# A hybrid decoder trunk on one core: square roots and inverse square roots move from Newton steps on VectorE to a power operation on GpSimd

## The chip, the cores and the metric

The kernel runs on one core of one Trainium2 chip. The metric is the device time of one execution, in microseconds (us). Engines carry the profile's names: PE (TensorE, matrix products), DVE (VectorE), ACT (ScalarE), POOL (GpSimd) and SP (SyncE, which starts most DMAs); PEld is the loading of weights into PE.

## The reference

Two layers over 16 meta tokens and 512 sequence tokens with 1024 channels, all in float32. Each layer is a feed-forward block, a mixer of three parallel groups that share one input and one output projection, and a second feed-forward block, each followed by a normalization. The places with a square root or its inverse are these:

```python
def _layer_norm(x, g, b):
    mu = jnp.mean(xf, axis=-1, keepdims=True)
    var = jnp.mean(jnp.square(xf - mu), axis=-1, keepdims=True)
    return (xf - mu) * lax.rsqrt(var + LN_EPS) * g + b
def _rms_norm(x, w):
    return xf * lax.rsqrt(jnp.mean(xf * xf, axis=-1, keepdims=True) + RMS_EPS) * w
def _l2norm(x):
    return x * lax.rsqrt(jnp.sum(x * x, axis=-1, keepdims=True) + RMS_EPS)
# _rg_lru_group, for each of 256 channels and every token
    a = jnp.exp(log_a)
    b = jnp.sqrt(-jnp.expm1(2.0 * log_a)) * (i * u)
    _, h = lax.associative_scan(_linear_combine, (a, b), axis=1)
# one layer
    h = _layer_norm(ALPHA * h + 0.5 * _swiglu(h, ...), ...)
    lru, ssd, dn = split(h @ w_in)
    mix = concatenate([_rg_lru_group(lru), _ssd_group(ssd), _deltanet_group(dn)]) @ w_out
    h = _layer_norm(ALPHA * h + mix, ...)
    h = _layer_norm(ALPHA * h + 0.5 * _swiglu(h, ...), ...)
```

The state-space group ends in an rms norm, the delta group l2-normalizes its q and k and ends in an rms norm, and the recurrent group (RG-LRU) takes the square root of a whole array.

## The kernel before

Activations lie with channels on the 128 partitions and tokens along the free dimension. The tokens are cut into two units: u=0 with 272 tokens (16 meta and 256) and u=1 with 256. Every large product is done as three float32r products of high and low parts (`hh`, `hl` for activations, `wt` for weights). A weight slab of 128x1024 arrives by DMA in `wr` (3 buffers), ACT writes its high part into `wt` (6 buffers), and the low part is a subtraction, for about 70% of the mixer's slabs and the shared feed-forward slabs in four parts on POOL (`wt<-wr,wt 128x256`), otherwise in one piece on DVE (`wt<-wr,wt 128x1024`). Products land in PSUM tiles `g` (3 buffers), all small products in PSUM tiles `c` (5 buffers).

Nothing is issued while the program is written down. A `Recorder` collects every operation with what it reads and writes, prices it (`price`, line 117), and `schedule` (line 233) sets one order for each engine: of the operations that are ready, the one with the longest priced path to the end goes first. `issue` then emits that order, so nearly all instructions carry line 390 in the profile and are told apart by their tiles. Each engine is handed its instructions in that order; what it needs from another engine it waits for with a semaphore, and what stands behind a waiting instruction on DVE or POOL waits with it. A POOL operation with two inputs is priced, whatever its arithmetic, at `148 + 2.1 * n` ns for n elements per partition (line 150): 719 ns for 272.

The two units are staggered, so that the mixer of one runs beside the feed-forward block of the other (`weave`). In the profile the stretches from about 300 to 900 us and from about 1560 to 2200 us hold the mixers of layers 0 and 1; the rest is almost pure feed-forward.

`rsqrt` (line 782) is eleven DVE instructions: two integer instructions on the bits for a first guess, then three Newton rounds of three instructions, each depending on the one before. It is called 42 times, on these tiles:

- `lv` in `layer_norm` (10 calls; 3 elements per partition). Behind it PE spreads the result over the partitions, and all 8 pieces of `acc` are scaled by it.
- `d_ss` in `dn_pre` (10 calls; 4 or 2 elements), followed by a product with `s0`, which makes a square root; it scales `v`.
- `d_sq` in `dn_finish` (4 times two calls in a row; 12 elements for u=0 and 8 for u=1), then spread by PE over the delta group's output.
- `s_sv` in `ssd_finish` (4 calls; 6 or 4 elements).
- `lru` in `lru` (8 calls: 2 layers, 2 units, 2 halves k; 272 or 256 elements). The argument is `r`, the guess is in `th`, and the scratch is the tile `l_h`, so that the Newton rows read `l_h<-lru`, `l_h<-l_h,lru` and `lru<-l_h,lru`. A POOL product with `r` makes the square root, then DVE forms the gated input (`lru<-lru`) and scans it (`l_h<-lru`, into `l_h`). The working tile `lru` has one buffer, so the second half starts when the first is done.
- `frs` in `final_tile` (2 calls; 2 elements), for the last normalization, done in rows.

`dn_finish`, `ssd_finish` and the two halves of `lru` all stand ahead of a unit's output projection, which reads all three groups. Below, these four stretches (two layers, two units) are called the finishes. `softplus`, a helper for other places, computes log(1+e) with a series of about a dozen DVE instructions.

Of the kernel before, what the change touches and what calls it, by code (L numbers as in the profile page):

```python
# [10 lines left out]
I32 = mybir.dt.int32  # L11
# [4 lines left out]
P = 128  # L16
# [383 lines left out]
class Trunk:  # L400
# [29 lines left out]
    def consts(self):  # L430
        nc, ins = self.nc, self.ins
        self.ident = self.tl(self.cp, [P, P], "ident")
        nc.gpsimd.memset(self.ident, 0.0)
        nc.gpsimd.affine_select(self.ident, self.ident, compare_op=ALU.not_equal, fill=1.0, base=0, pattern=[[-1, P]], channel_multiplier=1)
        self.hh = [self.tl(self.hp, [P, KD, n], f"hh{u}", F32R) for u, n in enumerate(NTOK)]
        self.hl = [self.tl(self.hp, [P, KD, n], f"hl{u}", F32R) for u, n in enumerate(NTOK)]
        self.acc = [None, None]
        self.res = [self.tl(self.dr, [P, KD, n], f"res{u}") for u, n in enumerate(NTOK)]
        self.par = self.tl(self.cp, [P, NROW], "par")
        self.ones = self.tl(self.cp, [P, P], "ones")  # L440
        nc.gpsimd.memset(self.ones, 1.0)
        nc.idle = self.ones
        self.tri = self.tl(self.cp, [P, P], "tri")
        nc.gpsimd.affine_select(self.tri, self.ones, pattern=[[1, P]], compare_op=ALU.is_ge, fill=0.0, base=0, channel_multiplier=-1)
        self.bd = self.block_ones(64, "bd")
        self.bdtri = self.tl(self.cp, [P, P], "bdtri")
        nc.gpsimd.tensor_tensor(self.bdtri, self.tri, self.bd, ALU.mult)
        self.tri2 = self.fold(self.bdtri, "tri2")
        self.eye2 = self.fold(self.ident, "eye2")
        self.mask = []  # L450
        for k in (16, 32):
            m = self.block_ones(2 * k)
            v = m.rearrange("p (b c) -> p b c", c=2 * k)
            nc.gpsimd.memset(v[:, :, :k], 0.0)
            nc.gpsimd.affine_select(m, m, pattern=[[2 * k, P // (2 * k)], [0, 2 * k]], compare_op=ALU.is_ge, fill=0.0, base=k - 1, channel_multiplier=-1)
            self.mask.append(self.fold(m, f"mask{k}"))
        self.bd16 = self.fold(self.block_ones(16), "bd16")
        self.pm = self.tl(self.cp, [P, 1], "pm")
        nc.vector.tensor_reduce(self.pm, self.eye2[:, 0:META], axis=AX.X, op=ALU.add)
        self.halo = self.tl(self.cp, [P, 14, 3], "halo")  # L460
        self.lcar = self.tl(self.cp, [P, 2], "lcar")

# [316 lines left out]
        assert f0 == NF  # L779
        return shared, alone  # L780

    def rsqrt(self, y, v, tmp):

        nc = self.nc
        nc.vector.tensor_scalar(y.bitcast(I32), v.bitcast(I32), 1, None, ALU.logical_shift_right)
        nc.vector.tensor_scalar(y.bitcast(I32), y.bitcast(I32), -1, 0x5F3759DF, ALU.mult, ALU.add)
        for _ in range(3):
            nc.vector.tensor_tensor(tmp, y, y, ALU.mult)
            nc.vector.scalar_tensor_tensor(tmp, tmp, -0.5, v, ALU.mult, ALU.mult)
            nc.vector.scalar_tensor_tensor(y, tmp, 1.5, y, ALU.add, ALU.mult)  # L790

    def layer_norm(self, u, s, row, off=0, keep=False):

# [33 lines left out]
            nc.vector.tensor_scalar(v[:, 0, 1:nb], vp[:, 1:nb], 1.0 / D, LN_EPS, ALU.mult, ALU.add)  # L827
        else:
            nc.vector.tensor_scalar(v[:, 0, :nb], vp[:, :nb], 1.0 / D, LN_EPS, ALU.mult, ALU.add)
        self.rsqrt(v[:, 1, :], v[:, 0, :], v[:, 2, :])  # L830
        rp = self.tl(self.psm, [P, 512], "c")[:, :n]
        for i, (c, w) in enumerate(blocks):
            nc.tensor.matmul(rp[:, c:c + w], v[:w, 1, i:i + 1].to_broadcast([w, P]), self.ident[:w, :w], start=True, stop=True)
# [171 lines left out]
    def dn_pre(self, u, bi, st):  # L1005
# [42 lines left out]
        nc.vector.tensor_scalar(tmp, cb, -1.0, None, ALU.mult)  # L1048
        nc.vector.tensor_tensor(nn, nn, tmp.unsqueeze(3).to_broadcast([P, 2, nch, 64]), ALU.mult)
        nc.gpsimd.tensor_tensor(kq[:, :, :, 1], kq[:, :, :, 1], eg, ALU.mult)  # L1050
        self.rsqrt(irk, s0, tmp)
        nc.vector.tensor_tensor(irk, irk, s0, ALU.mult)
        dn = self.tl(self.dr, [2, 16448], "d_nd", bufs=3)
        for h in range(2):
            dst = dn[h, :16384].rearrange("(a j c t) -> a j c t", j=2, c=2, t=64)
# [155 lines left out]
    def dn_finish(self, l, u, st):  # L1211
        nc = self.nc
        n = NTOK[u]
        bl = self.blocks(u)
        nb = len(bl)
        sq = st["sq"]
        ot = [st["big"][:, 6 + p, :n] for p in range(2)]
        qs = []
        for p in range(2):
            q = self.tl(self.wk, [P, 272], "lq")[:, :n]  # L1220
            nc.scalar.activation(q, ot[p], AF.Square)
            qs.append(q)
        po = self.tl(self.psm, [P, 512], "c")
        for p in range(2):
            for bi, (o, w) in enumerate(bl):
                nc.tensor.matmul(po[:w, bi * 4 + 2 * p:bi * 4 + 2 * p + 2], qs[p][:, o:o + w], self.bd[:, 0:128:64], start=True, stop=True)
        for bi, (o, w) in enumerate(bl):
            nc.vector.tensor_copy(sq[:w, bi, 1], po[:w, bi * 4:bi * 4 + 4])
        T = lambda i: sq[:, :nb, i]
        rq, a2, tmp = T(2), T(3), T(4)  # L1230
        nc.vector.tensor_scalar(T(0), T(0), RMS_EPS, None, ALU.add)
        self.rsqrt(rq, T(0), tmp)
        nc.vector.tensor_scalar(rq, rq, 0.125, None, ALU.mult)
        nc.vector.tensor_tensor(a2, rq, rq, ALU.mult)
        nc.vector.scalar_tensor_tensor(a2, a2, 1.0 / 64, T(1), ALU.mult, ALU.mult)
        nc.vector.tensor_scalar(a2, a2, RMS_EPS, None, ALU.add)
        self.rsqrt(T(0), a2, tmp)
        nc.vector.tensor_tensor(rq, rq, T(0), ALU.mult)
        for p in range(2):
            rb = self.bcast_rows(u, lambda bi, w: [sq[:w, bi, 2, 2 * p + h:2 * p + h + 1] for h in range(2)])  # L1240
            nc.vector.scalar_tensor_tensor(ot[p], ot[p], self.col(ROW_DNW + l), rb, ALU.mult, ALU.mult)
        for p in range(2):
            nc.vector.tensor_tensor(ot[p], ot[p], st["gate"][p], ALU.mult)
            self.out_split(u, 6 + p, ot[p])
# [82 lines left out]
    def ssd_finish(self, l, u, st):  # L1327
# [13 lines left out]
            for bi, (o, w) in enumerate(bl):  # L1341
                nc.tensor.matmul(po[:w, bi * 2 + g:bi * 2 + g + 1], q[0][:, o:o + w], self.ones[:, 0:1], start=True, stop=True)
        sv = self.tl(self.mx, [P, 3, 3, 2], "s_sv", bufs=2)
        v, y, tmp = (sv[:, i, :nb] for i in range(3))
        nc.vector.memset(v, 1.0)
        for bi, (o, w) in enumerate(bl):
            nc.vector.tensor_scalar(v[:w, bi], po[:w, bi * 2:bi * 2 + 2], 0.25 / 256, RMS_EPS, ALU.mult, ALU.add)
        self.rsqrt(y, v, tmp)
        for g in range(2):
            rb = self.bcast_rows(u, lambda bi, w: [sv[:w, 1, bi, g:g + 1]])  # L1350
            for j in (2 * g, 2 * g + 1):
# [3 lines left out]
    def lru(self, l, u, k, uc):  # L1355
# [18 lines left out]
        nc.gpsimd.tensor_tensor(r, a, a, ALU.mult)  # L1374
        nc.vector.scalar_tensor_tensor(r, r, 1.0, th, ALU.add, ALU.mult)
        nc.vector.tensor_scalar(r, r, -1.0, 1e-37, ALU.mult, ALU.max)
        self.rsqrt(th, r, uc)
        nc.gpsimd.tensor_tensor(r, r, th, ALU.mult)
        nc.vector.scalar_tensor_tensor(i, i, 0.5, r, ALU.mult, ALU.mult)
        nc.vector.tensor_tensor_scan(uc, a, i, 0.0 if u == 0 else self.lcar[:, k:k + 1], ALU.mult, ALU.add)  # L1380
        if u == 0:
# [167 lines left out]
    def final_tile(self, u, m):  # L1549
# [15 lines left out]
        if m < KD - 1:  # L1565
            return
        v = self.tl(self.wk, [P, 2, 2], "fmv")
        w = self.tl(self.wk, [P, 4, 2], "frs")
        for b in range(2):
            nc.vector.bn_aggr(v[:, b], st[:, b])  # L1570
        var, r, t, mr = (w[:, i] for i in range(4))
        nc.vector.tensor_scalar(var, v[:, :, 1], LN_EPS, None, ALU.add)
        self.rsqrt(r, var, t)
        g, o = self.gb[:, :D], self.gb[:, D:]
        nc.vector.scalar_tensor_tensor(mr, v[:, :, 0], -1.0, r, ALU.mult, ALU.mult)
        nc.scalar.activation(x[1], x[1], AF.Identity, scale=r[:, 1:2], bias=mr[:, 1:2])
# [64 lines left out]
```

## Time and profile before

| | us |
|---|---|
| median of 3 runs | 2460.74 (2446.69 to 2464.13) |
| the profiled execution's own time | 2460.38 |
| span of its trace | 2458.7 |
| busy: PE, DVE | 2312.6, 1504.2 |
| busy: ACT, POOL | 865.9, 883.0 |

The span reaches from the first to the last instruction; 1.7 us of the profiled execution's time lie around it. Busy shares are averages over stretches with different limits, and a busy PE is not PE at its peak.

### The profile page before, as it was taken

To read this page: it belongs to the slowest core of one execution; us is meant where nothing else is said; L and a number is where in the kernel's file an instruction comes from. 1 tells how busy PE (TensorE), PEld (TensorE's weight loads), DVE (VectorE), ACT (ScalarE), POOL (GpSimd) and SP (SyncE) were. 2 spreads that over 40 slices of the span, in tenths; PEclk is the share of its full clock that TensorE was granted. 3 is DMA by queue.
4 is the path that set the end of the run, shared out by engine and by line. 5 is a ranking of instruction groups with operands and counts; after the bars stand their busy time and mean duration, and the time that the engine had idled before them with its cause. 6 is when DMAs were issued, how large, how long until landed. Compare 5 with 4: busy or idle time off the path is not lost.

```text
span 2458.7 us, 46832 instructions
## 1 busy us (share of the span) xinstructions
PE 2312.6 (94%) x18712; PEld 2199.1 (89%) x18712; DVE 1504.2 (61%) x3529; ACT 865.9 (35%) x1546; POOL 883.0 (36%) x1214
## 2 busy tenths in 40 slices
PE   8999998988899999999999999998989989999997
PEld 8999998876887999999999999988768878999996
DVE  6444467757867664444574444678577686654445
ACT  3222344442333454222242223443433444432222
POOL 5000566634545576000010005666445556640000
PEclk9999999987886999999999999999888989999999
DMA  6232454531341456233232334545314525552320
GB/s 169 78 103 87 131 145 144 146 97 35 110 108 54 139 157 186 86 104 95 68 95 80 91 91 138 156 139 141 97 35 118 142 61 155 172 168 90 91 90 35
DMA packets 426332, 271.99 MB, mean 111 GB/s; under 512 B 33421, under 2 KB 407921, under 8 KB 425857
## 3 DMA queue, kind: packets, MB, share of 16 engines
q1 hardware_dynamic: 425536, 268.83, 37.7%
q8 instruction: 147, 2.41, 0.4%
q0 software_dynamic: 576, 0.16, 0.1%
q14 instruction: 73, 0.59, 0.1%
HBM read 260.76 MB, written 8.19 MB: 109 GB/s over the span
## 4 chain that ended last, share of the span: by engine, by line
PE 70%; DVE 16%; DMA 4%; issue 3%; POOL 3%; ACT 3%; SPq 0%; POOLq 0%; DVEq 0%; ACTq 0%
PE g L390 61%; PE c L390 9%; POOL wt L390 2%; DVE wt L390 2%; DVE acc L390 2%; DVE fs L390 1%; DVE lru L390 1%; ACT wt L390 1%; DMA wr<-in_ffn_w_gate_dram 1%; DVE d_sq L390 1%; DVE s L390 1%; DMA wr<-in_ffn_w_up_dram 1%; DMA d_tx<-d_xd 1%; DVE sp L390 1%; DVE l_h L390 1%
## 5 line engine op out<-in xcount | busy, mean ns | idle before, releaser
L390 PE MATMUL g<-hh,wt 128*128 128x256 f32 (+1 forms) x7616 | 1063.7, 290 | 22.5 <-DVE fs L390 8.8
L390 PEld LDWEIGHTS g<-hh,wt 128*128 128x128 f32 x7616 | 985.4, 192 | 37.5 <-DVE fs L390 9.0
L390 POOL TENSOR_TENSOR wt<-wr,wt 128x256 fp32r<-128x256 f32 x884 | 681.8, 803 | 783.7 <-ACT wt L390 726.4
L390 ACT CAST wt<-wr 128x1024 fp32r<-128x1024 f32 x484 | 498.0, 1040 | 619.0 <-PE g L390 482.0
L390 PE MATMUL g<-hl,wt 128*128 128x256 f32 (+1 forms) x3808 | 562.7, 288 | 1.8 <-DVE hl L390 1.2
L390 PE MATMUL g<-hid,wt 128*128 128x256 f32 (+1 forms) x4224 | 543.7, 286 | 18.6 <-DVE hid L390 10.2
L390 PEld LDWEIGHTS g<-hid,wt 128*128 128x128 f32 x4224 | 524.4, 189 | 27.2 <-DVE hid L390 13.0
L390 PEld LDWEIGHTS g<-hl,wt 128*128 128x128 f32 x3808 | 505.3, 192 | 6.3 <-DVE hl L390 2.5
L390 DVE SCALAR_TENSOR_TENSOR acc<-g,acc 128x256 f32<-128x256 f32 (+1 forms) x608 | 256.7, 427 | 226.1 <-PE g L390 222.0
L390 DVE TENSOR_TENSOR wt<-wr,wt 128x1024 fp32r<-128x1024 f32 x263 | 335.0, 1285 | 88.1 <-ACT wt L390 86.8
L390 DVE SCALAR_TENSOR_TENSOR fs<-ft,g 128x272 f32<-128x272 f32 (+1 forms) x200 | 84.6, 423 | 188.8 <-ACT ft L390 188.0
L390 DVE TENSOR_TENSOR g<-fs,g 128x256 f32<-128x256 f32 (+1 forms) x176 | 76.4, 434 | 173.9 <-PE g L390 173.5
L390 ACT ACTIVATE ft<-g 128x272 f32<-128x272 f32 (+1 forms) x208 | 80.6, 388 | 281.6 <-PE g L390 249.2
L390 ACT CAST hid<-g 128x256 fp32r<-128x256 f32 (+1 forms) x176 | 65.8, 374 | 223.5 <-DVE g L390 223.2
L390 POOL TENSOR_TENSOR ls<-ls,lq 128x256 f32<-128x256 f32 (+1 forms) x30 | 27.6, 920 | 264.2 <-ACT lq L390 261.3
L390 DVE TENSOR_TENSOR hid<-g,hid 128x256 fp32r<-128x256 f32 (+1 forms) x176 | 74.9, 425 | 42.4 <-ACT hid L390 42.1
L390 POOL TENSOR_TENSOR wr<-wr,db 128x512 f32<-128x512 f32 x4 | 5.0, 1274 | 262.0 <-ACT wr L390 262.0
L390 DVE SCALAR_TENSOR_TENSOR fs<-g,par,fs 128x271 f32<-128x271 f32 (+1 forms) x144 | 69.1, 482 | 21.9 <-ACT halo L390 17.0
L390 ACT ACTIVATE fs<-g,par 128x272 f32<-128x272 f32 (+1 forms) x48 | 25.2, 524 | 67.4 <-PE g L390 57.9
L390 DVE SCALAR_TENSOR_TENSOR acc<-acc,par,c 128x256 f32<-128x256 f32 (+1 forms) x104 | 43.6, 480 | 8.6 <-PE c L390 8.5
L390 ACT ACTIVATE ft<-fs 128x272 f32<-128x272 f32 (+1 forms) x56 | 23.7, 423 | 58.6 <-DVE fs L390 58.6
L390 POOL TENSOR_TENSOR s<-s,s_sm 128x512 f32<-128x512 f32 (+1 forms) x20 | 22.0, 1105 | 61.6 <-ACT s L390 45.1
(305 smaller groups left out, 1742.4 us busy)
## 6 DMA issues: line engine op xcount, KB each, us to landing
wr<-in_ffn_w_gate_dram SPq DMA_DIRECT2D x120, 512.0 KB
wr<-in_ffn_w_up_dram SPq DMA_DIRECT2D x120, 512.0 KB
wr<-in_ffn_w_down_dram SPq DMA_DIRECT2D x120, 512.0 KB
wr<-in_w_in_dram SPq DMA_DIRECT2D x88, 512.0 KB
wr<-in_w_out_dram SPq DMA_DIRECT2D x32, 512.0 KB
res<-acc SPq DMA_DIRECT2D x2, 1088.0 KB
acc<-res SPq DMA_DIRECT2D x8, 272.0 KB
acc<-in_x_dram SPq DMA_DIRECT2D x4, 512.0 KB
```

The lines of the kernel that those rows point to most:

```text
L390: op.fn(*[on(x) for x in op.args], **{k: on(x) for k, x in op.kw.items()})
```

## The change

`rsqrt` is gone. `power` is one POOL instruction with two inputs: the argument, and a tile `half` that holds the exponents 0.5 and -0.5 in its two columns, one of them repeated along the free dimension. The inverse square roots take -0.5. The two places that multiplied an inverse square root by its argument to get a square root (`d_ss` and `lru`) take 0.5 and drop that product, which was a DVE instruction in `dn_pre` and a POOL instruction in `lru`. Prices and rules of the `Recorder` are the same, so the power is priced like any POOL operation with two inputs.

```diff
+        self.half = self.tl(self.cp, [P, 2], "half")
+        nc.gpsimd.memset(self.half[:, 0:1], 0.5)
+        nc.gpsimd.memset(self.half[:, 1:2], -0.5)
...
-    def rsqrt(self, y, v, tmp):
-
-        nc = self.nc
-        nc.vector.tensor_scalar(y.bitcast(I32), v.bitcast(I32), 1, None, ALU.logical_shift_right)
-        nc.vector.tensor_scalar(y.bitcast(I32), y.bitcast(I32), -1, 0x5F3759DF, ALU.mult, ALU.add)
-        for _ in range(3):
-            nc.vector.tensor_tensor(tmp, y, y, ALU.mult)
-            nc.vector.scalar_tensor_tensor(tmp, tmp, -0.5, v, ALU.mult, ALU.mult)
-            nc.vector.scalar_tensor_tensor(y, tmp, 1.5, y, ALU.add, ALU.mult)
+    def power(self, y, v, e):
+
+        t = self.half[:, 0 if e > 0 else 1:][:v.shape[0], 0:1]
+        for _ in v.shape[2:]:
+            t = t.unsqueeze(2)
+        self.nc.gpsimd.tensor_tensor(y, v, t.to_broadcast(list(v.shape)), ALU.pow)
...
-        self.rsqrt(v[:, 1, :], v[:, 0, :], v[:, 2, :])
+        self.power(v[:, 1, :], v[:, 0, :], -0.5)
...
-        self.rsqrt(irk, s0, tmp)
-        nc.vector.tensor_tensor(irk, irk, s0, ALU.mult)
+        self.power(irk, s0, 0.5)
...
-        self.rsqrt(rq, T(0), tmp)
+        self.power(rq, T(0), -0.5)
...
-        self.rsqrt(T(0), a2, tmp)
+        self.power(T(0), a2, -0.5)
...
-        self.rsqrt(y, v, tmp)
+        self.power(y, v, -0.5)
...
-        self.rsqrt(th, r, uc)
-        nc.gpsimd.tensor_tensor(r, r, th, ALU.mult)
+        self.power(r, r, 0.5)
...
-        self.rsqrt(r, var, t)
+        self.power(r, var, -0.5)
```

The order that the planner sets is new on every engine, since it depends on the prices. Two places show it. The numbers behind a tile's name only tell buffers apart; they are one higher after the change, because `half` was allocated ahead of them.

DVE before, in the finish of layer 0, u=0: the second half of the LRU (`lru`, `l_h_950`) with the delta group's norm (`d_sq`) and the state-space group's (`s_sv`).

```order
L390 SCALAR_TENSOR_TENSOR lru_944<-l_h_950,lru_944 128x272
L390 TENSOR_SCALAR d_sq_653<-d_sq_653 128x3x4
L390 TENSOR_TENSOR s_sv_1036<-s_sv_1036 128x6
L390 TENSOR_TENSOR l_h_950<-lru_944 128x272
L390 TENSOR_SCALAR d_sq_653<-d_sq_653 128x3x4
L390 SCALAR_TENSOR_TENSOR s_sv_1036<-s_sv_1036 128x6
L390 SCALAR_TENSOR_TENSOR l_h_950<-l_h_950,lru_944 128x272
L390 SCALAR_TENSOR_TENSOR fs_138<-g_139,par_103,fs_138 128x256
L390 SCALAR_TENSOR_TENSOR lru_944<-l_h_950,lru_944 128x272
L390 SCALAR_TENSOR_TENSOR fs_138<-g_139,par_103,fs_138 128x256
```

The Newton rounds of the three tiles are dealt out in turn, one instruction of each, with a convolution row (`fs`) between.

DVE after, at the same place, from the instruction that ends the LRU's argument (`TENSOR_SCALAR lru`) on.

```order
L390 TENSOR_SCALAR lru_945<-lru_945 128x272
L390 TENSOR_TENSOR d_sq_654<-d_sq_654 128x3x4
L390 MEMSET s_sv_1037 128x6
L390 SCALAR_TENSOR_TENSOR d_sq_654<-d_sq_654 128x3x4
L390 TENSOR_SCALAR s_sv_1037<-c_125 16x2
L390 TENSOR_SCALAR s_sv_1037<-c_125 128x2
L390 SCALAR_TENSOR_TENSOR fs_148<-ft_138,g_146 128x272
L390 TENSOR_SCALAR s_sv_1037<-c_125 128x2
L390 TENSOR_SCALAR d_sq_654<-d_sq_654 128x3x4
L390 SCALAR_TENSOR_TENSOR lru_945<-lru_945 128x272
L390 TENSOR_TENSOR d_sq_654<-d_sq_654 128x3x4
L390 SCALAR_TENSOR_TENSOR l_h_951<-lru_945 128x272
```

The rounds are gone. The instruction that reads the root (`SCALAR_TENSOR_TENSOR lru<-lru`) stands eight rows behind the one that ends its argument, and the second norm of `d_sq`, the scan into `l_h` and all that follows stand behind it.

POOL before, at the same place: weight parts, one product for the LRU (`lru`) and copies for the next unit (`mt`).

```order
L390 TENSOR_TENSOR wt_156<-wr_132,wt_156 128x256 x2
L390 TENSOR_TENSOR lq_577<-lq_577,lq_576 128x272
L390 TENSOR_TENSOR lru_944<-lru_944 128x272
L390 TENSOR_TENSOR wt_156<-wr_132,wt_156 128x256 x2
L390 COPY mt_719<-sm_623 16x128 x3
L390 TENSOR_TENSOR wt_158<-wr_120,wt_158 128x256 x4
L390 TENSOR_TENSOR wt_133<-wr_134,wt_133 128x256 x4
L390 TENSOR_TENSOR lru_944<-lru_944 128x272
L390 COPY lcar_118<-l_h_950 128x1
```

The LRU appears with a product ahead of its root and one behind it; the norms do not appear.

POOL after, at the same place.

```order
L390 TENSOR_TENSOR wt_134<-wr_133,wt_134 128x256 x2
L390 TENSOR_TENSOR d_sq_654<-d_sq_654,half_117 128x3x4
L390 TENSOR_TENSOR wt_134<-wr_133,wt_134 128x256
L390 TENSOR_TENSOR lru_945<-lru_945 128x272
L390 TENSOR_TENSOR lq_578<-lq_578,lq_577 128x272
L390 TENSOR_TENSOR wt_143<-wr_135,wt_143 128x256
L390 TENSOR_TENSOR lru_945<-lru_945,half_117 128x272
L390 TENSOR_TENSOR s_sv_1037<-s_sv_1037,half_117 128x6
L390 TENSOR_TENSOR d_sq_654<-d_sq_654,half_117 128x3x4
L390 TENSOR_TENSOR wt_143<-wr_135,wt_143 128x256 x2
L390 COPY lcar_119<-l_h_951 128x1
L390 TENSOR_TENSOR wt_143<-wr_135,wt_143 128x256
```

Rows with `half` are powers. The LRU's power of 272 elements stands directly ahead of the powers of `s_sv` and of the second `d_sq`, and behind these wait the weight parts.

## Rows read from the trace of the kernel before

**Rows 1.** The page, part 1: span, then busy us (share) and instructions of each engine.

```profile
span 2458.7 us, 46832 instructions
PE 2312.6 (94%) x18712; PEld 2199.1 (89%) x18712; DVE 1504.2 (61%) x3529; ACT 865.9 (35%) x1546; POOL 883.0 (36%) x1214
```

**Rows 2.** The page, part 4: shares of the span on the chain that ended last, by engine.

```profile
PE 70%; DVE 16%; DMA 4%; issue 3%; POOL 3%; ACT 3%; SPq 0%; POOLq 0%; DVEq 0%; ACTq 0%
```

**Rows 3.** The chain in the four finishes, shares by tile: 586-626, 786-822, 1815-1870, 1990-2045 us.

```profile
by line: DVE lru L390 25.0%; DVE d_sq L390 22.6%; DVE l_h L390 14.4%; issue 7.6%; DVE wt L390 5.9%; DVE fs L390 5.7%; POOL acc L390 4.2%; DVE s_sv L390 2.7%; PE c L390 2.5%; POOL lru L390 1.9%; DVE db L390 1.8%; DVE acc L390 1.7%; DVE s_st 
by line: PE g L390 24.9%; PE c L390 22.0%; DVE lru L390 10.6%; DVE d_sq L390 10.3%; DVE s_sv L390 8.3%; DVE l_h L390 8.0%; DVE wt L390 3.2%; PE g L388 3.0%; DVE lv L390 2.8%; issue 1.9%; DVE fs L390 1.7%; DVE ls L390 1.6%; DVE hid L390 1.0%
by line: PE g L390 28.7%; PE c L390 18.0%; DVE d_sq L390 13.1%; DVE lru L390 9.9%; DVE l_h L390 6.4%; DVE acc L390 4.1%; DVE wt L390 4.1%; DVE fs L390 3.6%; POOL wt L390 3.5%; ACT wt L390 1.7%; DVE db L390 1.7%; DVE s_sv L390 1.1%; DVE sp L
by line: DVE d_sq L390 13.3%; PE g L390 12.5%; DVE lru L390 12.2%; DVE l_h L390 11.5%; DVE acc L390 9.2%; DVE hl L390 8.7%; issue 6.6%; DVE lv L390 5.8%; DVE fs L390 5.2%; DVE wt L390 4.9%; ACT wt L390 1.9%; PE c L390 1.6%; DVE s_sv L390 1.
```

**Rows 4.** Waits of PE: tile waited for, us in total, times, longest.

```profile
PE c L390 <- DVE lv L390: 9.3, 6, 2.3
PE c L390 <- DVE d_sq L390: 4.4, 2, 3.2
PE c L390 <- DVE s_sv L390: 2.8, 2, 1.4
```

**Rows 5.** DVE groups of small calls: form, count, busy us, mean ns, idle before.

```profile
L390 DVE SCALAR_TENSOR_TENSOR lv<-lv 128x3 f32<-128x3 f32 x60 | 13.7, 229 | 1.2
L390 DVE TENSOR_TENSOR lv<-lv 128x3 f32<-128x3 f32 x30 | 6.8, 228 | 0.5
L390 DVE TENSOR_SCALAR lv<-lv 128x3 int32<-128x3 int32 x20 | 7.9, 397 | 0.4
L390 DVE SCALAR_TENSOR_TENSOR d_sq<-d_sq 128x12 f32<-128x12 f32 (+1 forms) x52 | 17.1, 328 | 0.3
L390 DVE TENSOR_TENSOR d_sq<-d_sq 128x12 f32<-128x12 f32 (+1 forms) x32 | 8.2, 255 | 0.2
L390 DVE TENSOR_SCALAR d_sq<-d_sq 128x12 int32<-128x12 int32 (+3 forms) x28 | 11.5, 412 | 0.1
L390 DVE SCALAR_TENSOR_TENSOR d_ss<-d_ss 128x4 f32<-128x4 f32 (+1 forms) x60 | 14.8, 260 | 0.4
L390 DVE TENSOR_TENSOR d_ss<-d_ss 128x4 f32<-128x4 f32 (+1 forms) x40 | 9.7, 256 | 0.4
L390 DVE TENSOR_SCALAR d_ss<-d_ss 128x4 f32<-128x4 f32 (+3 forms) x40 | 9.3, 253 | 0.1
```

**Rows 6.** DVE groups of the LRU's Newton steps, same columns.

```profile
L390 DVE SCALAR_TENSOR_TENSOR l_h<-l_h,lru 128x272 f32<-128x272 f32 (+1 forms) x24 | 12.9, 540 | 0.1
L390 DVE SCALAR_TENSOR_TENSOR lru<-l_h,lru 128x272 f32<-128x272 f32 (+1 forms) x24 | 12.3, 511 | 0.2
L390 DVE TENSOR_TENSOR l_h<-lru 128x272 f32<-128x272 f32 (+1 forms) x24 | 12.1, 505 | 0.4
L390 DVE TENSOR_SCALAR lru<-lru 128x272 f32<-128x272 f32 (+3 forms) x32 | 15.8, 493 | 1.6 <-ACT lru L390 1.5
```

**Rows 7.** POOL groups, same columns: weight parts, the LRU's products, a one-column copy.

```profile
L390 POOL TENSOR_TENSOR wt<-wr,wt 128x256 fp32r<-128x256 f32 x884 | 681.8, 803 | 783.7 <-ACT wt L390 726.4 <-PE g L390 34.4 <-issue 13.0
L390 POOL TENSOR_TENSOR lru<-lru 128x272 f32<-128x272 f32 (+1 forms) x16 | 12.3, 769 | 36.1 <-DVE lru L390 13.7 <-ACT lru L390 11.5 <-DVE d_sq L390 8.6
L390 POOL COPY lcar<-l_h 128x1 f32<-128x1 f32 x4 | 0.8, 204 | 3.3 <-DVE d_sq L390 2.6 <-DVE l_h L390 0.6
```

**Rows 8.** Timeline in the first finish: start us, duration us, engine, operation, count.

```profile
605.33 3.28 DVE L390 SCALAR_TENSOR_TENSOR lru<-lru 128x272 f32<-128x272 f32 x1
605.52 2.79 POOL L390 TENSOR_TENSOR wt<-wr,wt 128x256 fp32r<-128x256 f32 x4
```

**Rows 9.** Tile `lru` over the span: length, busy us (count) of DVE, ACT, POOL; clock, DMA.

```profile
0.00:2459.00 2459.00, 96.31 (x152) 14.64 (x32) 12.30 (x16) 0.95 0.38 111
```

**Rows 10.** All work from 600 to 700 us: length, busy of PE, PEld, DVE, ACT, POOL; clock.

```profile
600.00:700.00 100.00, 89.95 (x692) 84.56 (x691) 88.54 (x274) 41.36 (x84) 56.59 (x81) 0.90 0.43 117
```

More of the change, by code (lines that the diff above doesn't have):

```diff
@@ L1229, in dn_finish @@
         T = lambda i: sq[:, :nb, i]
-        rq, a2, tmp = T(2), T(3), T(4)
+        rq, a2 = T(2), T(3)
         nc.vector.tensor_scalar(T(0), T(0), RMS_EPS, None, ALU.add)
-        self.rsqrt(rq, T(0), tmp)
+        self.power(rq, T(0), -0.5)
         nc.vector.tensor_scalar(rq, rq, 0.125, None, ALU.mult)
@@ L1343, in ssd_finish @@
         sv = self.tl(self.mx, [P, 3, 3, 2], "s_sv", bufs=2)
-        v, y, tmp = (sv[:, i, :nb] for i in range(3))
+        v, y = (sv[:, i, :nb] for i in range(2))
         nc.vector.memset(v, 1.0)
@@ L1567, in final_tile @@
         v = self.tl(self.wk, [P, 2, 2], "fmv")
-        w = self.tl(self.wk, [P, 4, 2], "frs")
+        w = self.tl(self.wk, [P, 3, 2], "frs")
         for b in range(2):
             nc.vector.bn_aggr(v[:, b], st[:, b])
-        var, r, t, mr = (w[:, i] for i in range(4))
+        var, r, mr = (w[:, i] for i in range(3))
         nc.vector.tensor_scalar(var, v[:, :, 1], LN_EPS, None, ALU.add)
-        self.rsqrt(r, var, t)
+        self.power(r, var, -0.5)
         g, o = self.gb[:, :D], self.gb[:, D:]
```

## The prediction

> **What bounds the kernel now.** I read part 1 of the page first: PE is busy for 94% of the span, DVE for 61% and POOL for 36% [rows 1]. So only the time in which PE stands still or its work comes late can be won. The chain that ended last, next, is PE for 70% of the span and DVE for 16% [rows 2], so DVE work does lie on the path. Where, the chain by stretches shows: in the finishes, where a unit's three groups end ahead of the output projection [rows 3]. There the tiles of the changed code carry large shares. Last come the waits of PE: it stands idle 9.3 us in all for `lv`, 4.4 for `d_sq` and 2.8 for `s_sv` [rows 4]. In the pure feed-forward stretches none of this bounds anything. In the stretch of the first finish DVE is busy 88.5 of 100 us and POOL 56.6 [rows 10].
>
> **What is removed.** For the small tiles I add up the groups of rows 5. `lv`: 13.7 + 6.8 + 7.9 = 28.4 us for 10 calls. `d_sq`: 48 of the 52, 24 of the 32 and 16 of the 28 instructions are Newton's, 15.8 + 6.2 + 6.6 = 28.6 us for 8 calls. `d_ss`: all of the first two groups and 20 of the 40 in the third, 14.8 + 9.7 + 4.7 = 29.2 us for 10 calls. `s_sv` and `frs` are 66 more instructions; at 0.23 us, the lowest mean of rows 5, 15 us for 6 calls. Together 101 us for 34 calls, 3.0 us each. For the LRU it is 12.9 + 12.3 + 12.1 and half of 15.8, 45.2 us for 8 calls, 5.65 us each [rows 6]. So DVE loses 146 us of its 1504, and POOL loses 8 products at 0.77 us [rows 7].
>
> **What of it lies on the path.** The four finishes of rows 3 are 40, 36, 55 and 55 us long. Share by length gives 9.0 + 3.7 + 7.2 + 7.3 = 27 us of chain for `d_sq`, 44 us for `lru` and `l_h` together (25.9 + 18.5), and about 5 us for `s_sv`. Of the `d_sq` rows about three quarters are Newton's (28.6 of 36.8 us), so 20 us. Of DVE's 96.3 us on the tile `lru` [rows 9], 45.2 are Newton's; `l_h` has other rows too, so I take two fifths of 44, 18 us. For `lv` I take what PE waits, 9.3 us. The small tiles then have 20 + 5 + 9.3 = 34 us on the path and the LRU 18. `d_ss` I cost at nothing: its root only scales `v`, and the block inverses through DRAM stand between that and its use; without that cover it would be worth a few us more.
>
> **What is added.** 42 POOL instructions that no trace here shows. Nearest are a one-column copy, 0.20 us, and a product of two inputs over 272 columns, 0.77 us [rows 7]; the second is the lower end for the LRU's power. A power done in software takes a logarithm, a product and an exponential. The kernel's own `softplus` spends about a dozen DVE steps on one logarithm; with as many for the exponential and some handling of bits I count up to 30 passes, and 30 at 0.77 us are 23 us, the upper end by rows. A loop that keeps its intermediate values in registers need not pay the loads and stores of 30 passes. Newton's 11 steps would be 8.5 us as POOL passes, and a general power does more than these. I take 12 us for 272 columns, between 8.5 and 23 and nearer the lower, which is 44 ns per column; 12 columns would then be about 0.7 us, 3 columns about 0.3 us.
>
> The Trainium skill has a rule that bears on this price (GPSIMD Engine Reference, Elementwise — side-by-side cycle accounting): a loop with three or more operations per element runs at roughly three operations a cycle. By it, 30 operations are 10 cycles of 1.2 GHz per column, an estimate of 2.3 us for 272 columns, and the sum would be that of the first rival. No run here shows it for more than one operation.
>
> **The small powers.** Power and hand-over: 0.3 to 0.7 us, and about half of a weight part that is already running, 0.4 of 0.8 us [rows 7]; 1.1 us in place of 3.0. On the path that turns 34 us into 13: a gain of 21 us. Both ends: nothing, if the power waits behind a whole slab of four parts (3.2 us), and 34 us, if it costs nothing.
>
> **The LRU's powers.** Here the order matters. The planner prices the power at 0.72 us, like a product, and places the DVE instruction that reads the root accordingly: in the piece of DVE's order shown, eight mostly small rows behind the end of the argument. In seven of the eight places there are only none to eight such rows, about 1.2 us of work on average; in one (layer 0, u=1, first half) about 9 us. Everything behind that reader on DVE stands too: the scan, the second `d_sq` norm, the accumulations from PSUM. On POOL, the powers of `s_sv` and `d_sq` and the weight parts queue behind the long power. At 12 us DVE stands for 7 x 10.8 + 3 = 79 us. Not all of it moves the end: DVE holds from under half to most of the chain in the finishes [rows 3], and I count two thirds, 52 us. Less the 18 us of Newton rows that leave, the LRU costs 34 us net.
>
> **The sum.** 2460.4 us of the profiled execution, which is 0.3 below the median of the runs, less 21, plus 34: 2474 us. The same sum with other prices of the LRU's power (each at two thirds): 0.77 us gives 2421, 5 us 2439, 8 us 2453, 18 us 2506, 23 us 2533. It is zero at about 9.5 us. So the whole forecast hangs on one number that the trace does not hold, and the change trades a certain gain at the small tiles for an open cost at the large one.
>
> **The rivals.**
>
> *The power is cheap*, a few passes: 0.8 to 5 us for 272 columns. For it speaks that a sum over one instruction has one load and one store, whereas Newton's eleven steps pay these eleven times: the `lv` steps take 0.23 us on three columns [rows 5]. Against it speaks that POOL takes 0.77 us for a single product, so that even one pass is slower than on DVE (0.50 to 0.54 us, rows 6). The times run from 2421 to 2439; I put it at 2428.
>
> *The power is dear*: one LRU power holds POOL for 23 us or more. It decides from about 14 us on, where 1% is lost, and at 23 us DVE stands 7 x 21.8 + 14 = 167 us; two thirds of that give 2533 and all of it 2588, since with POOL blocked that long the weight parts come late as well and PE has no other work. I put it at 2555. For it: a software power is the only POOL operation here that is not one simple arithmetic step. Against it: nothing in the trace; it would be odd only to plan such an instruction at 0.72 us.
>
> *POOL holds DVE off*, even from rows that need nothing of it. In the first finish a DVE instruction that reads two tiles in SBUF takes 3.28 us, where like instructions of the Newton steps take 0.54 [rows 6], and it spans four POOL weight parts of 2.79 us [rows 8]. If a power holds DVE off in the same way, the rows placed beside it no longer hide any of it: DVE stands 8 x 12 = 96 us for the LRU, two thirds of it 64 in place of 52, and the 34 small powers stop DVE for some 0.5 us each, 17 us of which I count two thirds. That is 2474 + 12 + 11 = 2497. The Trainium skill states this as a rule (SBUF — State Buffer, SBUF: two separate sides): a DVE instruction with two SBUF inputs and a POOL instruction that reads SBUF share a port pair, and whichever starts first blocks the other for its whole length. The trace agrees in this row; whether a power that mostly computes holds the port too, no run here shows.
>
> **How the numbers follow.** I give the forecast (a power of 5 to 18 us, the loss and the gain of like size) 0.37, the cheap power 0.31, the dear one 0.22 and the held-off DVE 0.10. The forecast's own range is 2439 to 2506. A measurement of this kernel can tell about 1% from no change, so the bounds are 2436 and 2485. Faster by more than that: 0.28 of the cheap case and 0.03 of the forecast, 0.31. Within: 0.20 of the forecast, 0.03 of the cheap case and 0.02 of the held-off one, 0.25. Slower: 0.14, 0.22 and 0.08, 0.44. The range for 8 in 10 runs from 2412, where all of the small tiles' 34 us goes and the LRU's power hides, to 2620, beyond 2588 since a power somewhat above 23 us is not excluded; a loop that works lane by lane would lie far above, and is most of what I leave out.
>
> **What would show it.** In the changed kernel's profile: a POOL group of 8 powers on `lru` with its mean, which settles the main term (12 us expected; under 5 the cheap rival, over 20 the dear one); POOL groups of powers on `lv`, `d_sq`, `d_ss` and `s_sv` of 0.3 to 0.7 us; DVE busy near 1360 us, more if it is held off; idle time of DVE ahead of `lru<-lru`, released by POOL, near 79 us in all; in the finishes `d_sq` gone from the chain; PE's waits for `lv` down to a third. The forecast is wrong in its main step if the LRU's power is under 5 us or over 18. It is wrong in its counting if the power is near 12 us and the time still moves by more than 2%, for then DVE's standing counts by much more or less than two thirds.

## The result, and the profile after

The changed kernel takes 2712.4 us (median of 4 runs, 2708.2 to 2721.9), the kernel before 2458.2 us beside it: a ratio of 1.1048, with a 95% interval of 1.1012 to 1.1084. By that ratio it is some 258 us slower, where the forecast was 14 us slower and the range ended at 2620 us.

The page of the changed kernel: part 1 (busy us, share, instructions), three rows of part 2 (tenths in 40 slices of the span) and the head of part 4 (the chain by engine).

```profile
span 2709.5 us, 46251 instructions
...
PE 2286.2 (84%) x18614; PEld 2179.7 (80%) x18614; DVE 1412.7 (52%) x3057; ACT 865.7 (32%) x1546; POOL 1255.0 (46%) x1250
...
PE   9999999843994499999999999999339834999997
...
POOL 4001776489558877000000026664887488860000
PEclk9999999875897699999999999998669867999999
...
PE 48%; POOL 16%; issue 14%; DVE 13%; DMA 5%; ACT 3%; SPq 0%; POOLq 0%; DVEq 0%; ACTq 0%
```

DVE lost 91.5 us of work [rows 1], and POOL, which had 3% of the chain [rows 2], now has 16%. PE was at nine tenths almost everywhere; now it is busy for only three to four tenths in slices 9 and 10, 13 and 14, 29 and 30, and 33 and 34. These are the four finishes. In them the granted clock is low as well, 0.5 to 0.7.

What POOL does there, in its groups of powers (form, count, busy us and mean ns, idle before), then the DVE group that reads the LRU's root and one that waited for another POOL product:

```profile
L390 POOL TENSOR_TENSOR lru<-lru,half 128x272 f32<-128x272 f32 x4 | 175.2, 43790 | 1.4 <-DVE s_sv L390 1.1 <-DVE lru L390 0.2
L390 POOL TENSOR_TENSOR lru<-lru,half 128x256 f32<-128x256 f32 x4 | 164.7, 41184 | 6.5 <-DVE lru L390 3.4 <-DVE d_sq L390 3.1
...
L390 POOL TENSOR_TENSOR d_sq<-d_sq,half 128x12 f32<-128x12 f32 x4 | 9.2, 2302 | 0.3 <-DVE d_sq L390 0.3
...
L390 POOL TENSOR_TENSOR lv<-lv,half 128x3 f32<-128x3 f32 x10 | 8.7, 872 | 7.5 <-DVE lv L390 7.5
...
L390 POOL TENSOR_TENSOR frs<-frs,half 128x2 f32<-128x2 f32 x2 | 1.4, 697 | 255.7 <-DVE frs L390 255.7
```

```profile
L390 DVE SCALAR_TENSOR_TENSOR lru<-lru 128x272 f32<-128x272 f32 (+1 forms) x16 | 11.8, 737 | 292.1 <-POOL lru L390 292.1
...
L390 DVE TENSOR_TENSOR fs<-ft,g 128x272 f32<-128x272 f32 (+1 forms) x8 | 3.4, 420 | 37.2 <-POOL acc L390 37.1
```

One power over 272 columns takes 43.8 us. The product that it stands for in the planner's prices took 0.77 us [rows 7], and the Newton steps that it replaces 5.65 us. DVE stood 292 us for POOL's `lru`, nearly all of it at seven of the eight roots, 39.9 to 42.5 us each. At the eighth (layer 0, u=1, first half) it stood ahead of the reader, 37.1 us for a product with `acc` that POOL had queued behind the power.

Did PE stand as well? A view by stretches of exactly the eight powers answers it (length; busy us and count of PE, PEld, DVE, ACT, POOL; clock; DMA); two of the stretches and the sum:

```profile
621.01:664.70 43.69, 1.10 (x10) 0.79 (x7) 1.27 (x7) 1.48 (x3) 43.69 (x1) 0.55 0.01 4
...
2183.05:2224.30 41.25, 1.09 (x10) 0.89 (x8) 0.23 (x2) 0.84 (x1) 41.25 (x2) 0.57 0.00 0
...
sum 339.83, PE 51.54 PEld 40.81 DVE 10.06 ACT 12.46 POOL 339.83; mean PE 6.44 PEld 5.10 DVE 1.26 ACT 1.56 POOL 42.48
```

PE works 51.5 of 339.8 us, so it is idle for 288 us; DVE and ACT, busy for 10.1 and 12.5 us, are nearly idle with it, and DMA too. The span grew by 251 us, so the rest of the program, together with these 51.5 us of PE's work, took some 37 us less than before. The granted clock in the stretches is 0.55 to 0.67, on average nearer to the lower of its two levels (0.5, 1.2 GHz) than to the upper. Three pieces in and behind the second power, same columns:

```profile
621.00:624.00 3.00, 1.11 (x10) 0.80 (x7) 1.28 (x8) 1.49 (x3) 2.99 (x1) 1.00 0.21 58
...
628.00:635.00 7.00, 0.00 (x0) 0.00 (x0) 0.00 (x0) 0.00 (x0) 7.00 (x1) 0.50 0.00 0
...
672.00:680.00 8.00, 8.00 (x37) 6.57 (x38) 2.21 (x5) 0.00 (x0) 3.00 (x7) 0.50 0.49 133
```

PE has no work from 624 us on, by 628 us the clock is at its lower level, and from 672 to 680 us PE is busy throughout and still runs at it. So part of what a hold costs is paid behind it.

What PE waited for, by tile (us in total, times, longest):

```profile
PE g L390 <- DVE fs L390: 80.7, 6, 39.9
PE c L390 <- POOL lq L390: 48.9, 3, 43.4
PE c L390 <- POOL s_sv L390: 44.9, 2, 44.0
PE g L390 <- DVE acc L390: 43.7, 11, 36.1
PE g L390 <- DVE hid L390: 41.2, 11, 35.2
PE c L390 <- POOL mt L390: 38.7, 1, 38.7
PE g L390 <- DVE hl L390: 37.3, 6, 35.3
```

Not one of these tiles is a root that is late by itself, except `s_sv`, whose own power is 1.3 us. They are what stood behind a long power in a queue. Taken power by power, PE's long wait is at four of the eight for a tile behind DVE's waiting reader (`fs` twice, `hid`, `acc`; 35.2 to 39.9 us), at three for one behind the power on POOL itself (`s_sv` 44.0, `lq` 43.4, `mt` 38.7 us), and at one for `hl` (35.3 us), in the place where DVE stood for POOL's `acc`. So there are two candidate mechanisms, DVE's wait and POOL's hold, and the profile of this kernel alone doesn't say which of them is needed.

### The profile page after: what moved, and what is told of

The parts are those of the page before. It is cut to its first block, busy times and chain, and to the rows that moved or that the text cites. A ratio compares the mean times of both kernels' runs of the same rounds, so it can differ in the third digit from the quotient of the medians.

```text
span 2709.5 us, 46251 instructions
## 1 busy us (share of the span) xinstructions
PE 2286.2 (84%) x18614; PEld 2179.7 (80%) x18614; DVE 1412.7 (52%) x3057; ACT 865.7 (32%) x1546; POOL 1255.0 (46%) x1250
## 4 chain that ended last, share of the span: by engine, by line
PE 48%; POOL 16%; issue 14%; DVE 13%; DMA 5%; ACT 3%; SPq 0%; POOLq 0%; DVEq 0%; ACTq 0%
PE g L390 41%; POOL lru L390 11%; PE c L390 7%; POOL wt L390 4%; DVE wt L390 2%; DVE acc L390 2%; DVE fs L390 2%; ACT wt L390 2%; DMA wr<-in_ffn_w_up_dram 1%; DVE hl L390 1%; DMA wr<-in_ffn_w_gate_dram 1%; DMA d_tx<-d_xd 1%; DMA wr<-in_ffn_w_down_dram 1%; DVE d_t L390 1%; DVE db L390 1%
## 5 line engine op out<-in xcount | busy, mean ns | idle before, releaser
L390 PEld LDWEIGHTS g<-hl,wt 128*128 128x128 f32 x3808 | 508.6, 193 | 44.9 <-DVE hl L390 38.9
L390 POOL TENSOR_TENSOR lru<-lru,half 128x272 f32<-128x272 f32 (+1 forms) x8 | 339.9, 42487 | 7.9 <-DVE lru L390 3.6
L390 DVE SCALAR_TENSOR_TENSOR lru<-lru 128x272 f32<-128x272 f32 (+1 forms) x16 | 11.8, 737 | 292.1 <-POOL lru L390 292.1
```

What stands on the lines that cost most here:

```text
L390: op.fn(*[on(x) for x in op.args], **{k: on(x) for k, x in op.kw.items()})
```

## The experiments

All are compared with the kernel before. Powers kept or added are the `power` of the change; "Newton" means the old `rsqrt` with its product.

**Only the small tiles.** The changed kernel with Newton for the LRU.

```diff
-        self.power(r, r, 0.5)
+        self.rsqrt(th, r, uc)
+        nc.gpsimd.tensor_tensor(r, r, th, ALU.mult)
```

> The changed kernel with one part undone: the LRU takes its square root with Newton steps on DVE and a POOL product as before, and all 34 small calls keep the power. Theory (the whole loss is the eight LRU powers of about 42 us, the small powers gain what the chain held of them, some 25 to 40 us): 2420 to 2435 us. Rival (the new order or the hand-overs between DVE and POOL cost what the small ones give): 2450 to 2470 us.

Measured: 2435.3 us, ratio 0.9913 (0.9883 to 0.9943), 21 us faster. The median is at the upper end of what the theory expected.

**Only the LRU.** The kernel before with those two lines replaced the other way round.

> The kernel before with the power in the LRU alone; all small calls keep Newton. Theory: the changed kernel's 2712 us plus the small ones' gain, 2735 to 2755 us. Rival (part of the loss is that the small powers queue behind the LRU's on POOL, and goes with them): 2690 to 2715 us.

Measured: 2760.2 us, ratio 1.1234 (1.1195 to 1.1274), 303 us slower, a little above the range of the theory, and the rival fell. The whole loss is the LRU's eight powers. The small powers are worth 48 us beside them (2760.2 against 2712.4; 46 us by the two ratios) and 21 us without. PE's waits (same columns) show where:

```profile
PE c L390 <- DVE s_sv L390: 130.8, 3, 46.6
...
PE c L390 <- DVE d_sq L390: 40.8, 2, 40.3
```

The Newton rows of these tiles stand on DVE behind the waiting reader; in the changed kernel PE's waits are 44.9 us for POOL's `s_sv` and 5.6 us for `d_sq`.

**The changed kernel with the power's measured price in the planner.**

```diff
+        if name == "tensor_tensor" and args[-1] == ALU.pow:
+            return 380 + 160 * n, 0
         return (120 + 3.33 * n if name == "tensor_copy" else 148 + 2.1 * n), 0
```

> The changed kernel, with the planner's price of a power set to what the trace shows: 380 ns and 160 ns per column, 43.9 us for 272, so that the order on every engine is made for it. Theory (a finish needs both roots one after the other, so the time stays on the path whatever the order): 2640 to 2700 us. Rival (the loss is that the planner took the power for 0.72 us and put its reader too early on DVE): under 2550 us.

Measured: 2697.7 us, ratio 1.0983 (1.0946 to 1.1020), in the range of the theory. The planner was told the truth, and 15 us came back of 258. DVE still stood 256 us for POOL's `lru` (292 in the changed kernel). So the wrong price in the planner accounts for no more than these 15 us. That too little work could go beside so long an instruction is my reading; no run tried an order by hand.

**Powers that nobody reads.** The kernel before, Newton and all; behind each of the LRU's eight scans POOL forms one power of 256 columns from two one-column inputs, and nothing uses it. It holds POOL as the change does, but no instruction waits for its result. The copy into `lcar`, which gives the power its input, is now made for both units, four copies more of 0.2 to 0.5 us.

```diff
-        if u == 0:
-            nc.gpsimd.tensor_copy(self.lcar[:, k:k + 1], uc[:, n - 1:n])
+        nc.gpsimd.tensor_copy(self.lcar[:, k:k + 1], uc[:, n - 1:n])
+        idle = self.tl(self.mx, [P, 256], "d_t")
+        nc.gpsimd.tensor_tensor(idle, self.half[:, 0:1].to_broadcast([P, 256]), self.lcar[:, k:k + 1].to_broadcast([P, 256]), ALU.pow)
```

> The kernel before, Newton everywhere, and eight added POOL powers of 256 columns (about 41 us each), one behind each LRU scan, whose results nobody reads. They hold POOL and make no engine wait for a result. Theory (the loss is DVE standing at the reader of the root): under 2500 us. Rival (a held POOL alone stops PE, since the weight parts come late): 2600 to 2700 us. If a power held DVE off as well, DVE rows beside it would stretch to its end.

Measured: 2724.8 us, ratio 1.1095 (1.1055 to 1.1135), 269 us slower. That DVE must wait for the root is therefore not needed for a loss of this size: holding POOL is enough. Of the two expectations the theory fell, and the rival's range was passed by 25 us. The waits of PE in this run (same columns) show through what:

```profile
PE c L390 <- POOL lq L390: 79.4, 4, 40.1
PE g L390 <- DVE acc L390: 46.5, 12, 36.8
PE c L390 <- DVE s_sv L390: 42.0, 4, 34.4
PE g L390 <- POOL wt L390: 38.9, 2, 20.5
PE g L390 <- ACT hh L390: 36.1, 3, 35.0
PE c L390 <- POOL mt L390: 27.8, 3, 26.6
```

These six add up to 271 us, of which `wt`, the weight parts, have 39. `lq`, `mt` and `wt` are POOL's own work, queued behind the power. `acc` and `s_sv` are DVE's, and DVE stands too, not for a power but for the ordinary products and the one-column copy that POOL has queued behind one (waits of DVE, same columns):

```profile
DVE lru L390 <- POOL lru L390: 71.8, 3, 37.4
DVE l_h L390 <- POOL lcar L390: 36.0, 1, 36.0
```

ACT's `hh` comes from the same copy. Behind DVE's 36.0 us for `lcar`, ACT stood 36.5 us for DVE's `l_h`, and the `hh` that PE waited 35.0 us for stands behind that row on ACT:

```profile
1994.31 0.47 ACT L390 ACTIVATE fs<-g,par 128x256 f32<-128x256 f32 x1 [36.54 <-DVE l_h L390]
```

The timeline of the first of these powers, weight parts and other instructions around it (start us, duration us, engine):

```profile
608.21 3.92 DVE L390 SCALAR_TENSOR_TENSOR lru<-lru 128x272 f32<-128x272 f32 x1
...
608.48 2.77 POOL L390 TENSOR_TENSOR wt<-wr,wt 128x256 fp32r<-128x256 f32 x4
...
611.22 41.16 POOL L390 TENSOR_TENSOR d_t<-half,lcar 128x256 f32<-128x256 f32 x1
...
614.00 0.42 DVE L390 SCALAR_TENSOR_TENSOR l_h<-l_h,lru 128x272 f32<-128x272 f32 x1
...
619.66 0.43 DVE L390 TENSOR_TENSOR hl<-l_h,hh 128x272 fp32r<-128x272 f32 x1
...
652.37 2.07 POOL L390 TENSOR_TENSOR wt<-wr,wt 128x256 fp32r<-128x256 f32 x3
654.41 0.75 POOL L390 TENSOR_TENSOR lru<-lru 128x272 f32<-128x272 f32 x1
```

For the first 10 us DVE works on as if nothing were there. Then what it needs is POOL's, and the next weight part and the next LRU product leave POOL only at 652 us.

Against this run, the one with only the LRU changed is 34 us slower still (2760.2 against 2724.8, intervals apart), although it has lost the Newton rows that I counted as 18 us of the path. Some 9 of the 34 us are longer powers (339.4 us in all against 330.5, half of them having 272 columns). The rest fits a waiting reader that adds to the hold; but the powers also stand at another place in POOL's order, ahead of the scan and not behind it, and no run separates the two.

**How long may POOL be held?** The same with 64 and with 128 columns, `[:, :64]` and `[:, :128]` of the same tile.

> As the kernel with unread powers, but of 64 columns, by the trace's 160 ns per column about 10.6 us each, 85 us of POOL in all. Theory (POOL held for longer than the weight buffers last stops PE; the buffers cover some 5 us of each): 8 x 5.6 = 45 us, 2490 to 2510 us. Rival (up to ten us are covered by the buffers): 2455 to 2470 us.

> The same with 128 columns, about 20.9 us each, 167 us in all. Theory: 8 x 15.9 = 127 us, 2570 to 2600 us, on a line with 64 and 256 columns. Rival (two slabs more are covered): 2520 to 2560 us.

Measured: 2488.8 us, ratio 1.0125 (1.0077 to 1.0172), and 2562.8 us, ratio 1.0413 (1.0366 to 1.0460). The first is just below the theory's range, the second between the two ranges. The groups of the powers, of 64 and then of 128 columns:

```profile
L390 POOL TENSOR_TENSOR d_t<-half,lcar 128x64 f32<-128x64 f32 x8 | 85.1, 10638 | 0.1
```

```profile
L390 POOL TENSOR_TENSOR d_t<-half,lcar 128x128 f32<-128x128 f32 x8 | 166.7, 20834 | 0.1
```

| one power holds POOL for | the eight cost | each costs | covered |
|---|---|---|---|
| 10.6 us | 31 us | 3.8 us | 6.8 us |
| 20.8 us | 102 us | 12.7 us | 8.1 us |
| 41.3 us | 269 us | 33.7 us | 7.6 us |

(The cost is the ratio less one, times 2459.5 us for the first two and 2459.0 for the third; "covered" is the length less the cost of each.) The intervals leave the cost of each open by 1.2 to 1.5 us either way. Within that, everything beyond 7 to 8 us of hold goes to the end in full, on the average of the eight places. The covered length is a net one, since it contains what the lower clock behind a hold costs.

**Which of the small tiles wins?** The kernel before with the power only in `layer_norm` (`lv`), only in the two norms (`d_sq`, `s_sv`), and only in `d_ss`:

```diff
-        self.rsqrt(v[:, 1, :], v[:, 0, :], v[:, 2, :])
+        self.power(v[:, 1, :], v[:, 0, :], -0.5)
```

> The kernel before with the power in the normalization of the residual (lv, 10 calls) alone. Theory (each small group gives what it holds of the path): PE waited 9.3 us for lv, two thirds of it go: 2450 to 2456 us. Rival (the gain of the small calls is all in the finishes, lv gives nothing): 2456 to 2462 us.

> The kernel before with the power in the two group norms at the finishes (d_sq and s_sv, 12 calls) alone. Theory: 25 us of chain, of which the powers of about 2 and 1.2 us leave half, so 2444 to 2450 us. Rival (a power of 2 us behind weight parts on POOL is no shorter a way than Newton's eleven steps dealt out on DVE): 2455 to 2462 us.

> The kernel before with the power in the delta group's l2 norm (d_ss, 10 calls) alone, the product behind it gone too. Theory (off the path): within 3 us of the kernel before, 2455 to 2461 us. Rival (29 us less on DVE in the mixer's dense stretches count): 2446 to 2453 us.

Measured: `lv` 2438.3 us, ratio 0.9928 (0.9901 to 0.9955), 18 us faster; the norms 0.9977 (0.9948 to 1.0005) and `d_ss` 0.9976 (0.9946 to 1.0006), some 6 us each, with intervals that reach no change. `lv` gave more than either expectation; the norms lie between theirs, and `d_ss` in the range of its rival, but neither is clear of noise. Most of the gain is the normalization's. Why so much, when PE's waits for `lv` were 9.3 us [rows 4]? Two pieces of the kernel before. First, who waited for the tile `lv` (us, times):

```profile
PEld c L390: 10.6, 6
PE c L390: 9.3, 6
```

Second, DVE's timeline in one normalization, from the statistics to the last Newton step:

```profile
1234.10 0.21 DVE L390 TENSOR_SCALAR lv<-c 128x2 f32<-128x2 f32 x2
...
1235.78 0.15 DVE L390 SCALAR_TENSOR_TENSOR lv<-lv 128x3 f32<-128x3 f32 x1
1235.93 0.42 DVE L390 SCALAR_TENSOR_TENSOR acc<-g,acc 128x256 f32<-128x256 f32 x1
1236.28 0.15 DVE L390 SCALAR_TENSOR_TENSOR lv<-lv 128x3 f32<-128x3 f32 x1
...
1240.30 0.15 DVE L390 SCALAR_TENSOR_TENSOR lv<-lv 128x3 f32<-128x3 f32 x1
```

Each step is 0.15 us, but rows of 0.4 us are dealt between, and from 1234.1 to 1240.5 the chain takes 6.4 us. With the power the same waits are:

```profile
PEld c L390: 4.7, 8
PE c L390: 2.8, 5
```

The weight load that reads `lv` waits on the same chain as the matmul behind it. Both together went from 19.9 to 7.5 us, but the two may overlap; the matmuls' waits alone fell by 6.5 us. And even these waits are not what the end won. The busy times of the run with the power in `lv`, whose span is 2434.2 us, say so:

```profile
PE 2290.4 (94%) x18654; PEld 2179.7 (90%) x18654; DVE 1492.6 (61%) x3419; ACT 866.5 (36%) x1546; POOL 902.1 (37%) x1226
```

PE's idle time, span less busy, is 143.8 us here and 146.1 us before [rows 1]: other waits took the place of those for `lv`. The spans differ by 24.5 us, and 22.2 of them are time in which PE is busy. (58 matmul records fewer, at 0.12 us, could be 7 of these.) PE got through the same work faster: the mean granted clock of this execution is 0.958, before it was 0.948; over all runs it is 0.957 on average of 12 against 0.951 of 35. Runs of the kernel before differ in the same way among themselves: the fastest of the 35, 2438.6 us, had 0.959, and the slowest, 2474.2 us, 0.943. On that scale 0.006 of clock is worth some 13 us, an estimate from these two runs. So the larger part of the gain came with a higher granted clock. The norms' and `d_ss`'s runs, at 0.953 and 0.956 on average, lie above 0.951 too. Why the clock was higher, these runs don't show.

**Can the small gain be made larger?** The small tiles with the planner's price right; then all small tiles but `d_ss`; then `lv` and `frs` alone:

```diff
-        self.rsqrt(r, var, t)
+        self.power(r, var, -0.5)
```

> All small calls by power, the LRU by Newton, as in the first experiment, and the planner's price of a power set to 380 ns and 160 ns per column (0.7 to 2.3 us in place of 0.15 to 0.17). Theory (the order places the readers right, DVE and PE stand less): 2425 to 2433 us. Rival (the price is too small a matter to change the time): 2432 to 2442 us, like the first experiment.

> Power in lv, d_sq, s_sv and frs; Newton in the LRU and in the delta group's l2 norm. Theory (gains of the single groups add up as far as the single runs showed them, d_ss gives little): 2432 to 2442 us. Rival (the powers of d_ss, behind which the weight parts wait, cost something in the full set): 2422 to 2432 us.

> Power in the two normalizations of the residual alone, lv and frs (12 calls, 2 or 3 columns). Theory (the gain of the small calls is nearly all here, and frs, the last thing of the program, adds about 1 us): 2435 to 2441 us. Rival (lv's gain in the single run was partly the luck of its order): 2444 to 2452 us.

Measured: 2443.8 us, ratio 0.9949 (0.9922 to 0.9977), with the right price; 2444.8 us, 0.9938 (0.9915 to 0.9962), without `d_ss`; 2433.5 us, 0.9900 (0.9869 to 0.9931), with `lv` and `frs` alone. The last is the fastest of all and beats both kernels, a little below its expected range, but its interval overlaps that of all the small tiles together (0.9913) and that of `lv` alone. The powers of the other small tiles neither help nor hurt beyond what these runs resolve, and the true price does not help either: that run is above both of its ranges, and the one without `d_ss` is too.

## Why the prediction was wrong

**The step that failed** is the price of the LRU's power: "I take 12 us for 272 columns, between 8.5 and 23 and nearer the lower". It is 43.8 us for 272 columns and 41.2 for 256, 42.5 on average. Neither bound held it: 30 passes at 0.77 us gave 23 us as the upper end. That end was no bound from rows but a count of steps that I had imagined for an operation, each at the price of the only simple one that the trace held. The text said that a loop working lane by lane would lie far above, and left that out of the range; the time lies there. Whether the power is such a loop, no run shows. The trace of before could have told only that nothing in it resembles a power, and the honest upper end was then open.

**The second term** is the share that moves the end, "I count two thirds". With the measured 42.5 us in the prediction's own sum, DVE stands 7 x 41.3 + 33.5 = 323 us. (Measured were 292, and 37 more for `acc`.) Two thirds of it, 215 us, less 18 and 21, give 2636 us, just above the range; all of it gives 2744. Measured are 2712, and PE was idle for 288 of the 340 us of the powers. So at this length nearly all of the standing counts, since what PE had in hand in the stretches was 1.1 to 12.0 us of work each. For a short hold the share is smaller: 3.8 of 10.6 us in the unread powers.

**The mechanism was half of it.** The place was right: DVE stood at the reader (292 us, expected 79 at 12 us each), and `fs`, `hid` and `acc` stood behind, as did the second norm where it was still Newton's. But the prediction made DVE's wait the path and POOL's queue an afterthought. The unread powers cost 269 us with no reader at all, so POOL's queue, with weight parts, `lq`, `mt` and the ordinary LRU products behind the power, carries a loss of the same size by itself. That there is a length up to which a power is free was right; by the three unread lengths it is 7 to 8 us (the forecast's zero, "at about 9.5 us", also held the gains), and beyond it each us counts, not two thirds.

**The small tiles** came out in sum (21 us forecast and measured) by errors that cancel. `lv` was put at 9.3 us of path, less a third that stays, and gave 18; the norms were put at 25 us of path, two thirds of which were to go, and gave about 6; `d_ss`, at nothing, gave 6 with an interval that reaches no change. So neither the share of a tile on the chain nor PE's waits for it said what is won when its rows go: for `lv` PE's idle time hardly changed, and the larger part of the gain came with the clock. For the norms PE's waits did not shrink at all, 4.4 and 2.8 us for `d_sq` and `s_sv` before [rows 4] and 3.8 and 3.6 with the power. The powers cost more than expected too, 0.87 us for 3 columns (0.3 forecast) and 2.3 us for 12 (0.7).

**The rivals.** The dear power happened, beyond the price of 23 us for which it was worked out. Its argument, that with POOL blocked PE has no other work, is what the unread powers show; but the late weight parts that it names were only 39 of 271 us there, and POOL's other work the rest. The cheap power fell. So did "POOL holds DVE off" as a term for the long powers: see the last section. By the Trainium skill (GPSIMD Engine Reference, Elementwise — side-by-side cycle accounting), roughly three operations a cycle, the estimate was 2.3 us for a count of 30 operations. The trace disagrees by a factor of 19, and the measurement decides; whether the rule or the count fails, no run shows. The range's lower end, 2412, is not quite what its terms give (2460.4 less 34 and 18 is 2408); nothing hangs on it.

**What was to show it.** DVE's busy time was 1412.7 us and not near 1360. Most of that error is at the small tiles: when the LRU keeps its Newton steps DVE is busy 1449.3 us, where 1504 less 101 would be 1403. The count of removed rows was right (3529 less 3145 instructions are 384, 34 times eleven and ten products), so the 46 us that were missed are not in the count. They have two parts of about equal size. The durations of DVE's groups add up to 1620.8 us before and 1546.7 in that run. The busy time is less, since neighbouring rows overlap: in the timeline of the normalization the row at 1235.93 us, 0.42 long, ends after the next has begun. So the forecast took durations from a busy time, and 19 us of the 74 that left the sum did not leave the busy time. And the removed rows add up to 99 us before, so those that stayed are longer by some 25 us, most of all two groups of `hl` (5.9 and 5.2 us). Why they are longer was not tried. As forecast, PE's waits for `lv` fell below a third, to 2.3 us, and DVE's `d_sq` is down to about 1% of the chain in the finishes.

## What to carry to other kernels

An operation that no trace holds should be measured by itself at its size before it is put into a kernel, and until then its upper bound is open. A long instruction holds up all that is queued behind it on its engine, even if nobody reads its result: here 7 to 8 us of each hold were covered, and all beyond went to the end. A short dependent chain on a busy engine lasts as long as the rows dealt between its steps, and replacing eleven steps by one instruction on another engine won 18 us here; but PE's waits for the chain did not tell that number, and a gain of this size should be split into idle time and clock before it is put down to a wait. It was won on tiles of a few columns only.

## What the runs showed of the hardware

The power on POOL takes about 0.38 us and 0.160 us for each column of 128 partitions: 0.697 us for 2 columns, 2.30 for 12, 10.6 for 64, 20.8 for 128, 43.8 for 272; (43.79 - 0.70) / 270 = 0.160. Powers of 0.5 and -0.5, and the unread ones whose exponent is data, lie on the same line.

These long powers did not hold DVE off. The last power of the changed kernel, and DVE's rows at its start:

```profile
2242.59 41.24 POOL L390 TENSOR_TENSOR lru<-lru,half 128x256 f32<-128x256 f32 x1 [3.38 <-DVE lru L390]
...
2242.76 0.84 DVE L390 TENSOR_TENSOR hl<-l_h,hh 128x256 fp32r<-128x256 f32 x1
2243.52 0.41 DVE L390 TENSOR_TENSOR hl<-acc,hh 128x256 fp32r<-128x256 f32 x1
```

Both rows read two tiles in SBUF and start after the power, and they end 40 us before it; the first takes twice as long as the second, but not as long as the power. In the run with unread powers, 0.42 and 0.43 us stand within 41.16 us, while just before a row of DVE is stretched to 3.92 us beside four weight parts of 2.77, as in [rows 8]. The Trainium skill (SBUF — State Buffer, SBUF: two separate sides) has the one that starts first hold the shared ports for its whole instruction. The rows with powers don't fit that. The rows with weight parts fit it in that the DVE row is blocked, but not in the order: by its start time the DVE row came first in both (605.33 us against 605.52 in [rows 8], 608.21 against 608.48 here), so the prediction's "the trace agrees in this row" holds for the blocking only. Why the two kinds of POOL instruction differ, these runs leave open.
